# Two-layer hybrid trunk step: the input projection by pairs of weight tiles, with 512 latent columns in one matmul

## The chip, the cores and the metric

One core of a Trainium2 chip runs the whole program, a step of two layers, in one launch. The metric is the device time in microseconds (us); lower is better. TensorE (PE) multiplies matrices from SBUF into PSUM, which has 8 banks of 512 fp32 values per partition; ScalarE (ACT), VectorE (DVE) and GpSimd (POOL) do the element-wise work, and SyncE (SP) issues most of the loads. Every engine runs its own instructions strictly in the order in which the program wrote them, and waits on semaphores for the others.

## What is computed

Each layer takes 640 tokens (128 of a new prompt, 512 latent ones) of width 2048, modulates them, projects them to 6656 columns, sends those through three branches (a bidirectional HGRN2 recurrence, windowed attention, a convolution module), gates them and projects back. Cut to what matters here:

```python
def trunk_layer(x, shift, scale, gate, w_in_l, w_out_l, ...):
    h = x * (1 + scale) + shift
    z = h @ w_in_l                                   # 2048 -> 6656
    aq, ak, av, ag, hq, hi, hff, hfb, hgate, ca, cb, cgate = split(z)
    att = attention(aq, ak, av)
    hg_out, s_fin = hgrn2_branch(hq, hi, hff, hfb, ...)
    cv_out = conv_branch(ca, cb, ...)                # GLU, 31 taps, LayerNorm, swish
    mix = concat([att * silu(ag), hg_out * silu(hgate), cv_out * silu(cgate)])
    return layer_norm(ALPHA * x + gate * (mix @ w_out_l))

def gates(hf, lb):                                   # in hgrn2_branch
    one_minus_f = (1 - lb) * sigmoid(-hf)
    logf = log1p(-minimum(one_minus_f, 1 - GATE_EPS))
    return one_minus_f, logf
# A = q k exp(G_t - G_s) in each chunk; the state goes on with k * exp(g_last - G)
```

`shift`, `scale` and `gate` come from `silu(c) @ ada_w`, a product of one vector per request with a matrix of 2048 x 6144 for each layer ("ada" below).

## The kernel before

The stream h lies in SBUF feature-major, split into two fp32r halves `HH` and `HL`. The 52 tiles of `w_in` (128 columns each, the list `NTILES`) are projected one after another: for each of the 16 slices k of the inner dimension three products (`wh` with HH, `wh` with HL, `wl` with HH), each as two matmuls with the same stationary weights, one over 256 columns (prompt and the first 128 latent tokens, L1173) and one over 384 (the other latent tokens, L1175), into a tile `z` of two PSUM banks. There are two such tiles and four single banks `m` for everything else. The result lies feature-major, 640 tokens wide, and one ScalarE activation empties it (`evac`): e_hf takes the sigmoid of a forget gate (L453) and then its Ln (L461), e_hi copies and transposes back to token-major, the others likewise.

The weights arrive in quarters of a tile (256 KB, SP queue), ScalarE writes their fp32r half and its negative (L290, L291), and a DMA of POOL adds the raw weights (`split_add`). These splits are written four quarters ahead of their use.

Nothing is scheduled at run time: Python generators (`active`) write the work of the branches, and between every two k slices of projection the program writes a few steps of them (`pump`). What a step writes on PE, ACT, DVE and POOL keeps this place for good. The layer begins with 16 tiles of HGRN2, head by head: `hff`, `hfb`, `hi`, `hq` of head j+1 are projected while the recurrence of head j (`hg_main`) is computed. Its part that matters here, in the order in which it stands: compact products on PE (L540), exponentials of the 8-step base for the two directions (L600 on DVE, then L602 and L603 on ACT), compact products of them (L540 again), exponentials for the chunk states (L636, L640, L644), transposes, two copies out of PSUM (L657), and the chunk-state matmuls (L664).

Layer 0 begins with a stretch in which the ada weights are streamed (`ada_pe`, 32 loads for scale and shift of both halves) while the first `NS` tiles are projected in steps of two k slices; the other ada products are formed on DVE between the projection's steps (L362), at `RATE` of them per step. Between the layers, the output projection of the last column group, the LayerNorm and the transposes of the next stream stand beside a first half of the next layer's first two tiles.

Of the kernel before, what the change touches and what calls it, by code (L numbers as in the profile page):

```python
# [45 lines left out]
WN = (0, 3, 4)  # L46
# [27 lines left out]
RATE = ((1.0, 0.85, 0.5, 1.2), (0.5, 0.5, 0.0, 0.8))  # L74
# [3 lines left out]
class Free:  # L78
# [8 lines left out]
    def put(self, *xs):  # L87
        self.f.extend(xs)

# [36 lines left out]
def trunk(ctx: ExitStack, tc: tile.TileContext, A: dict):  # L126
# [38 lines left out]
    zt = [psp.tile([P, 1024], F32, name=f"z{i}") for i in range(2)]  # L165
    mb = [psp.tile([P, 512], F32, name=f"m{i}") for i in range(4)]
    ZP = Free(zt)
    M = Free(mb)
# [55 lines left out]
    def zput(z):  # L224
        if isinstance(z, tuple):
            M.put(*z)
        else:
            ZP.put(z)

# [69 lines left out]
    def ada_pe(jobs, raws, after):  # L299
# [3 lines left out]
        for (part, nch), kq in tiles:  # L303
            while nxt < len(tiles) and raws:
                (p2, n2), k2 = tiles[nxt]
                r = raws.popleft()
                sync.dma_start(out=r, in_=A["adaw0"][p2, n2, k2])
                fly.append(r)
                nxt += 1
                if nxt == W0:  # L310
                    for i in range(NS):
                        w_load1(0, i, 0)
# [127 lines left out]
    def zsb(z):  # L440
        return z[:, 256:896]

    def e_hf(l, j, d, z):
# [9 lines left out]
        act.activation(kd, zsb(z), AF.Sigmoid, scale=-1.0)  # L453
        zput(z)
# [16 lines left out]
    def to_tokens(vT, v):  # L471
        b0 = yield from M.get()
        for c in range(4):
            pe.transpose(b0[:, 128 * c:128 * c + 128], vT[:, 128 * c:128 * c + 128], ident)
        act.copy(v[:, 0:512], b0)
        M.put(b0)
        b1 = yield from M.get()
        pe.transpose(b1[:, 0:128], vT[:, 512:640], ident)
        act.copy(v[:, 512:640], b1[:, 0:128])
        M.put(b1)  # L480

    def e_hi(l, j, z):
# [3 lines left out]
        if isinstance(z, tuple):  # L486
            act.copy(s[:, 0:256], z[0][:, 256:512])
            act.copy(s[:, 256:640], z[1][:, 0:384])
        else:
            act.copy(s[:, 0:T], zsb(z))  # L490
        zput(z)
        yield
        yield
        yield from to_tokens(s[:, 0:T], v)
        S.put(s)
        flags.add(("hi", l, j))

    def e_hq(l, j, z):
        yield from wait(("hgset", l, j))
        act.activation(hv(l, hgset[l, j])[2], zsb(z), AF.Silu)  # L500
        zput(z)
        flags.add(("hq", l, j))
        yield
# [244 lines left out]
    def e_ak(l, g, z):  # L748
# [5 lines left out]
        act.copy(kp, z[:, 256:384])  # L754
# [4 lines left out]
        act.copy(lat(s), z[:, 384:896].rearrange("p (a b) -> p a b", a=2))  # L759
        zput(z)  # L760
# [15 lines left out]
    def e_av(l, g, z):  # L776
        yield from wait(("hgdone", l, 2 + g), ("cache", l))
        s, vl = yield from S.getn(F32, F32R)
        act.copy(s[:, 0:T], zsb(z))
        zput(z)  # L780
# [7 lines left out]
        for c in range(4):  # L788
            pe.transpose(b[:, 128 * c:128 * c + 128], s[:, 128 + 128 * c:256 + 128 * c], ident)
        split(V[:, 0:512], vl[:, 0:512], b)  # L790
        M.put(b)
        b = yield from M.get()
        pe.transpose(b[:, 0:128], s[:, 0:128], ident)
        act.copy(vp, b[:, 0:128])
        M.put(b)
        S.put(s)
        pool.dma_start(out=A["nv"][l, g], in_=vp)
# [10 lines left out]
    def e_aq(l, h, z):  # L808
# [3 lines left out]
        act.copy(pq(l, h), z[:, 256:384])  # L812
        act.copy(s[:, 0:512], z[:, 384:896])
        zput(z)
# [185 lines left out]
    def e_cb(l, j, z):  # L1000
        s = yield from S.get()
        act.activation(s[:, 0:T], zsb(z), AF.Sigmoid)
        zput(z)
# [4 lines left out]
    def e_ca(l, j, z):  # L1008
# [6 lines left out]
        dve.tensor_tensor(u[:, 15:143], z[:, 256:384], s[:, 0:128], op=ALU.mult)  # L1015
        dve.tensor_tensor(u[:, 158:670], z[:, 384:896], s[:, 128:640], op=ALU.mult)
        zput(z)
# [76 lines left out]
    def e_gate(l, k, z):  # L1094
        s = yield from S.get()
        act.activation(s[:, 0:T], zsb(z), AF.Silu)  # L1096
        zput(z)
# [17 lines left out]
    wraw = {}  # L1115

    def w_load1(l, i, c):
        pump_until(lambda: RAW.f)
        r = RAW.take()
        sync.dma_start(out=r, in_=A["win"][l, i, c])  # L1120
        wraw[l, i, c] = r

    def w_load(l, i):
        for c in range(4):
            w_load1(l, i, c)
# [3 lines left out]
    def w_split(l, i, c, lo_eng=None, hi_eng=None):  # L1129
        pump_until(lambda: len(WH.f) >= 2)  # L1130
        hi, lo = WH.take(), WH.take()
        r = wraw.pop((l, i, c))
        if lo_eng == "dma":
            split_add(hi, lo, r, A["win"][l, i, c])
        else:
            split(hi, lo, r, lo_eng, hi_eng)
        wsp[l, i, c] = (hi, lo)
# [24 lines left out]
    def mm(l, i, z, ks, halves):  # L1162
        za, zb = (z[0][:, 256:512], z[1][:, 0:384]) if isinstance(z, tuple) else (z[:, 256:512], z[:, 512:896])
        za = za.rearrange("p (a b) -> p a b", b=P)
        zb = zb.rearrange("p (a b) -> p a b", b=P)
        for k in ks:
            hi, lo = wsp[l, i, k // 4]
            o = 128 * (k % 4)
            wh, wl = hi[:, o:o + 128], lo[:, o:o + 128]
            for n_, (w_, h_) in enumerate(((wh, HH), (wh, HL), (wl, HH))):  # L1170
# [8 lines left out]
    zs = [zt[0], zt[1], (mb[2], mb[3])]  # L1179
    M.f = deque(mb[0:2])  # L1180
    ZP.f.clear()
    for k in range(6):
        load_x0(k)
    def start_mm(n):
        for i in range(NS):
# [427 lines left out]
```

## Time and profile before

| | |
|---|---|
| time, median of 3 runs | 2254.14 us (2252.49 to 2255.09) |
| the profiled execution: its own time | 2252.99 us |
| its span in the trace | 2251.1 us |
| mean granted TensorE clock | 0.992 |
| PE busy | 97% (15854 instructions) |
| DVE, ACT, POOL busy | 65%, 51%, 27% |
| DMA, mean over the span | 179 GB/s |

The span is the time from the first to the last instruction in the trace of one profiled execution; 1.9 us of that execution's own time lie outside it. An engine's busy share counts the time in which at least one of its instructions ran. TensorE's matmuls overlap one another, so the duration of one in a row is longer than its distance to the next; distances between starts are what adds up.

### The profile page before, as it was taken

The numbers are of one execution on the slowest core, as the hardware profiler recorded it, in microseconds if no ns is written. First come the engines' busy times: TensorE is split into PE (matmuls) and PEld (weight loads), VectorE is DVE, ScalarE is ACT, GpSimd is POOL, SyncE is SP. The second block draws the span as 40 slices with busy tenths as digits, with TensorE's granted clock in tenths as the row PEclk, the third lists the DMA queues.
The fourth block names the chain that finished last, engine by engine and source line by source line (L and its number), as shares of the span: only waits on it lengthen the run. The fifth ranks groups of instructions, "written<-read, shape, count | busy, mean of one in ns | idle before, by whom it ended". The sixth has DMA issues, their size and how long they took to land.

```text
span 2251.1 us, 42122 instructions
## 1 busy us (share of the span) xinstructions
PE 2178.7 (97%) x15854; PEld 2077.2 (92%) x15854; DVE 1472.3 (65%) x3795; ACT 1142.6 (51%) x2047; POOL 616.0 (27%) x704
## 2 busy tenths in 40 slices
PE   6899999999999999999989999999999999999995
PEld 3699999999999999988989999999999999998895
DVE  2488889557669998676673666534655877234458
ACT  1177877546565335511165878764556543551111
POOL 0034334332222243300032344433222133330005
PEclk9999999999999999999999999999999999999998
DMA  9978787887777789964435777788776577685332
GB/s 371 400 191 203 184 200 188 206 218 182 170 159 170 190 193 229 272 197 135 118 130 135 160 173 163 158 193 186 162 153 129 114 170 157 144 196 178 96 97 103
DMA packets 210716, 403.60 MB, mean 179 GB/s; under 512 B 24816, under 2 KB 30672, under 8 KB 209872
## 3 DMA queue, kind: packets, MB, share of 16 engines
q1 hardware_dynamic: 138992, 271.85, 38.3%
q0 software_dynamic: 61600, 116.96, 30.3%
q10 hardware_dynamic: 9920, 12.10, 1.7%
q8 instruction: 124, 2.03, 0.4%
q14 instruction: 80, 0.66, 0.1%
HBM read 383.46 MB, written 12.11 MB: 176 GB/s over the span
## 4 chain that ended last, share of the span: by engine, by line
PE 77%; DVE 11%; DMA 4%; issue 3%; ACT 3%; POOL 1%; ACTq 0%; SPq 0%; DVEq 0%; POOLq 0%
PE z L1175 31%; PE z L1173 21%; PE z L1432 9%; PE m L1432 8%; DVE junk L362 4%; DMA x<-adaw 2%; PE m L948 2%; PE m L862 2%; PE m L916 1%; DMA s<-xT 1%; PE m L664 1%; DVE y1y L1414 1%; ACT s L1392 1%; DVE s L534 1%; DVE y1y L1415 0%
## 5 line engine op out<-in xcount | busy, mean ns | idle before, releaser
L1175 PE MATMUL z<-HH,wh 128*128 128x384 f32 x3296 | 1045.8, 338 | 0.0
L1173 PE MATMUL z<-HH,wh 128*128 128x256 f32 x3296 | 926.4, 283 | 1.6 <-DVE wh L287 0.9
L292 POOL DMA_DIRECT2D wh<-win x388 | 344.4, 933 | 1090.8 <-ACT wh L291 1021.5
L1173 PEld LDWEIGHTS z<-HH,wh 128*128 128x128 f32 x3296 | 619.4, 189 | 5.5 <-DVE wh L287 1.6
L1175 PEld LDWEIGHTS z<-HH,wh 128*128 128x128 f32 x3296 | 620.0, 188 | 1.5
L1175 PE MATMUL z<-HL,wh 128*128 128x384 f32 x1648 | 557.6, 338 | 0.0
L362 DVE SCALAR_TENSOR_TENSOR junk<-raw,s 128x256 bf16<-128x256 f32 x1024 | 503.8, 492 | 52.1 <-DMA raw<-adawD 24.4
L1173 PE MATMUL z<-HL,wh 128*128 128x256 f32 x1648 | 461.3, 280 | 0.0
L1173 PEld LDWEIGHTS z<-HL,wh 128*128 128x128 f32 x1648 | 311.0, 189 | 0.0
L1175 PEld LDWEIGHTS z<-HL,wh 128*128 128x128 f32 x1648 | 309.9, 188 | 0.0
L291 ACT ACTIVATE wh<-wh 128x512 fp32r<-128x512 f32 x400 | 253.1, 633 | 79.4 <-PE z L1175 68.4
L290 ACT CAST wh<-raw 128x512 fp32r<-128x512 f32 x400 | 244.0, 610 | 71.2 <-issue 36.2
L286 ACT CAST wh<-raw 128x512 fp32r<-128x512 f32 x136 | 83.0, 621 | 305.0 <-PE m L1432 156.6
L1027 DVE SCALAR_TENSOR_TENSOR s<-s,sm,s 128x655 f32<-128x655 f32 x240 | 231.2, 963 | 6.3
L1432 PE MATMUL z<-wh,HH 128*128 128x512 f32 (+1 forms) x640 | 182.0, 368 | 0.0
L1432 PE MATMUL m<-wh,HH 128*128 128x512 f32 (+1 forms) x640 | 173.8, 357 | 0.0
L287 DVE TENSOR_TENSOR wh<-raw,wh 128x512 fp32r<-128x512 f32 x138 | 92.6, 687 | 122.9 <-ACT wh L286 120.2
L1432 PEld LDWEIGHTS z<-wh,HH 128*128 128x128 f32 x640 | 116.1, 189 | 20.0
L1432 PEld LDWEIGHTS m<-wh,HH 128*128 128x128 f32 x640 | 114.1, 189 | 17.5
L1432 PE MATMUL z<-wh,HL 128*128 128x512 f32 (+1 forms) x320 | 117.7, 368 | 0.0
L1432 PE MATMUL m<-wh,HL 128*128 128x512 f32 (+1 forms) x320 | 114.3, 357 | 0.0
L1096 ACT ACTIVATE s<-z 128x640 f32<-128x640 f32 x32 | 22.5, 703 | 151.6 <-PE z L1175 142.8
(555 smaller groups left out, 2745.2 us busy)
## 6 DMA issues: line engine op xcount, KB each, us to landing
raw<-win SPq DMA_DIRECT2D x416, 256.0 KB, 4.2
wh<-win POOLq DMA_DIRECT2D x388, 256.0 KB, 5.5
raw<-adawD SPq DMA_DIRECT2D x256, 256.0 KB, 4.0
x<-adaw SPq DMA_DIRECT2D x64, 512.0 KB, 8.3
raw<-wout SPq DMA_DIRECT2D x128, 256.0 KB, 2.8
s<-crow SPq DMA_DIRECT2D x32, 256.0 KB, 5.9
s<-xT ACTq DMA_DIRECT2D x16, 320.0 KB, 7.1
s<-s ACTq DMA_DIRECT2D x80, 64.0 KB, 3.8
```

The source lines that it names most:

```text
L286: act.copy(hi, src)
L287: (lo_eng or dve).tensor_tensor(lo, src, hi.bitcast(F32), op=ALU.subtract)
L290: act.copy(hi, r)
L291: act.activation(lo, hi.bitcast(F32), AF.Copy, scale=-1.0)
L292: pool.dma_start(out=lo, in_=w.bitcast(F32R), accum_op=ALU.add)
L362: dve.scalar_tensor_tensor(junk, r[:, 256 * n:256 * n + 256], 1.0, rows[0][:, 256 * c:256 * c + 256], op0=ALU.mult, op1=ALU.mult, accum_ou ...
L862: pe.matmul(b[:, 0:w], lhsT=a_, rhs=k_, start=(n_ == 0), stop=(n_ == 2))
L948: pe.matmul(o, lhsT=v_, rhs=p_, start=(y == 0 and n_ == 0), stop=(y == len(bl) - 1 and n_ == 2))
L1027: dve.scalar_tensor_tensor(acc, u[:, t:t + AW], sm[:, cw + t:cw + t + 1], acc, op0=ALU.mult, op1=ALU.add)
L1173: pe.matmul(za, lhsT=w_, rhs=h_[:, 0:2, k, :], start=st_, stop=sp_)
L1175: pe.matmul(zb, lhsT=w_, rhs=h_[:, 2:5, k, :], start=st_, stop=sp_)
L1432: pe.matmul(bs[tt][:, 0:w], lhsT=h_[:, tt, k, :], rhs=w_[:, o:o + w], start=(k == 0 and n_ == 0), stop=(k == KT - 1 and n_ == 2))
```

## The change

The 52 tiles become 26 pairs. For each k slice and product there are now three matmuls: one over all 512 latent columns for each tile of the pair (L1228), and one of 256 columns for both tiles' prompt part, in which the prompt tokens (`HH[:, 0, k]`) are the stationary operand and the weights of both tiles are streamed (L1231). So the prompt comes out token-major. `Pair.fill` copies those 256 columns out of PSUM on ACT (L243), and two steps later PE transposes each tile's half back (L249), but for `hi` and `av`, which want it token-major anyway. Every evacuation is written twice, for 512 latent and 128 prompt columns. PSUM is one queue of 8 banks. The weights are packed by quarters of two k slices and 256 columns. Layer 0 starts with two pairs beside the ada stream (before: three tiles), layer 1 with one pair; two entries of RATE rise.

```diff
-RATE = ((1.0, 0.85, 0.5, 1.2), (0.5, 0.5, 0.0, 0.8))
+RATE = ((1.0, 0.85, 0.6, 1.3), (0.5, 0.5, 0.0, 0.8))
+    class Pair:
+        def fill(self):
+            cs = yield from S.get()
+            act.copy(cs[:, 0:256], self.c)
+            self.cput()
+            yield
+            yield
+            self.T = yield from M.get()
+            for t in self.need:
+                pe.transpose(self.T[:, 128 * t:128 * t + 128], cs[:, 128 * t:128 * t + 128], ident)
...
     def e_hf(l, j, d, z):
...
-        act.activation(kd, zsb(z), AF.Sigmoid, scale=-1.0)
-        zput(z)
+        act.activation(kd[:, 128:T], z.lat, AF.Sigmoid, scale=-1.0)
+        z.put_lat()
+        zp = yield from z.prompt()
+        act.activation(kd[:, 0:128], zp, AF.Sigmoid, scale=-1.0)
+        z.put()
...
-    def mm(l, i, z, ks, halves):
...
-                if 0 in halves:
-                    pe.matmul(za, lhsT=w_, rhs=h_[:, 0:2, k, :], start=st_, stop=sp_)
-                if 1 in halves:
-                    pe.matmul(zb, lhsT=w_, rhs=h_[:, 2:5, k, :], start=st_, stop=sp_)
+    def mm(l, p, z, ks, parts=(0, 1), lat=((1, 5),)):
...
+                if 1 in parts:
+                    for t in range(2):
+                        for a, b in lat:
+                            x = z.ab[t][:, 128 * (a - 1):128 * (b - 1)].rearrange("p (a b) -> p a b", b=P)
+                            pe.matmul(x, lhsT=w_[:, o + 128 * t:o + 128 * t + 128], rhs=h_[:, a:b, k, :],
+                                      start=st_, stop=sp_)
+                if 0 in parts:
+                    pe.matmul(z.c, lhsT=h_[:, 0, k, :], rhs=w_[:, o:o + 256], start=st_, stop=sp_)
-    NS = 3
+    NS = 2
...
-            mm(l + 1, 0, zt[0], range(KT), (0,))
+            head, rest = ((1, 3),), ((3, 5),)
+            mm(l + 1, 0, zs[0], range(8), lat=head)
             g = ln_next(TT - 1)
...
-            mm(l + 1, 1, zt[1], range(KT), (0,))
...
+            mm(l + 1, 0, zs[0], range(8, KT), lat=head)
+            for q in range(8):
+                mm(l + 1, 0, zs[0], (2 * q, 2 * q + 1), (1,), rest)
```

How this moves instructions is seen in the order in which they stand on an engine. On PE, in the steady part of layer 0 (before; z is the tile's PSUM pair, wh a quarter of the weights):

```order
L1173 MATMUL z_100<-HH,wh_235 128x256
L1175 MATMUL z_100<-HH,wh_235 128x384
L1173 MATMUL z_100<-HH,wh_238 128x256
L1175 MATMUL z_100<-HH,wh_238 128x384
L1173 MATMUL z_100<-HL,wh_238 128x256
L1175 MATMUL z_100<-HL,wh_238 128x384
```

and the same place of the changed kernel, where m_103 and m_99 are the latent banks of the two tiles and m_102 holds the prompt of both:

```order
L1228 MATMUL m_103<-HH,wh_314 128x512
L1228 MATMUL m_99<-HH,wh_314 128x512
L1231 MATMUL m_102<-wh_314,HH 128x256
L1228 MATMUL m_103<-HL,wh_314 128x512
L1228 MATMUL m_99<-HL,wh_314 128x512
```

Two tiles took four matmuls for a product, and now take three; in all PE has 14646 matmuls before and 12326 after, of which 92 are the new transposes L249, while the 12 that turned the prompt of `hi` and `av` are gone.

On ACT, in layer 1, while the recurrence of head 1 is computed and the gates of head 2 are emptied, between the exponentials of the chunk states and the copies L657 (before):

```order
L636 ACTIVATE s_8731<-h11gg 128x128 x4
L640 ACTIVATE s_12631<-h11gg 128x128 x4
L453 ACT_TABLE_LOAD
L453 ACTIVATE h10kt<-z_100 128x640
L290 CAST wh_235<-raw_246 128x512
L291 ACTIVATE wh_238<-wh_235 128x512
L644 ACT_TABLE_LOAD
L644 ACTIVATE aE_87<-h11gg 128x5
L645 ACTIVATE aE_87<-h11gg 128x5
L649 DMA s_9444<-st 128x128
L650 DMA s_7282<-st 128x128
L461 ACT_TABLE_LOAD
```

and in the changed kernel, where L680 and L684 are the old L636 and L640, L501 the sigmoid of a prompt part and L509 the Ln:

```order
L680 ACT_TABLE_LOAD
L680 ACTIVATE s_8286<-h11gg 128x128 x4
L501 ACT_TABLE_LOAD
L501 ACTIVATE h10kt<-m_106 128x128
L339 CAST wh_311<-raw_166 128x512
L340 ACTIVATE wh_418<-wh_311 128x512
L684 ACT_TABLE_LOAD
L684 ACTIVATE s_11425<-h11gg 128x128 x4
L509 ACT_TABLE_LOAD
L509 ACTIVATE s_11426<-s_11426 128x640
L501 ACT_TABLE_LOAD
L501 ACTIVATE h10kt<-m_106 128x128
```

Both gates of a head come out at the same time now, so their sigmoids and Lns stand between the exponentials. From the first base exponential (L602, now L646) to the copies (L657, now L701) ACT has 3 table loads before and 8 after, in five of the eight heads; for head 0 of layer 0 and for both heads 3 it has 6, and before 3 (2 for heads 3).

On PE, at the end of a layer's projection, before the first matmuls of the output projection (before: L1173 and L1175, then L1432):

```order
L1173 MATMUL z_99<-HH,wh_416 128x256
L1175 MATMUL z_99<-HH,wh_416 128x384
L1432 MATMUL m_101<-wh_417,HH 128x512
L1432 MATMUL m_101<-wh_617,HH 128x512
L1432 MATMUL m_101<-wh_417,HL 128x512
```

and now:

```order
L1228 MATMUL m_102<-HH,wh_6687 128x512
L1228 MATMUL m_106<-HH,wh_6687 128x512
L1231 MATMUL m_99<-wh_6687,HH 128x256
L249 MATMUL m_104<-ident,s_8286 128x128 x2
L1495 MATMUL m_105<-wh_6715,HH 128x512
```

The last pair's two transposes stand between the projection and the output matmuls (L1495), and they read what ACT copies out of PSUM after the pair's last matmul.

## Rows read from the trace of the kernel before

**Rows 1.** Page, busy time, share of the span and instructions of each engine.

```profile
PE 2178.7 (97%) x15854; PEld 2077.2 (92%) x15854; DVE 1472.3 (65%) x3795; ACT 1142.6 (51%) x2047; POOL 616.0 (27%) x704
```

**Rows 2.** Page, chain of work that ended last: shares of the span by engine.

```profile
PE 77%; DVE 11%; DMA 4%; issue 3%; ACT 3%; POOL 1%; ACTq 0%; SPq 0%; DVEq 0%; POOLq 0%
```

**Rows 3.** PE's waits: for what, us in total, times, longest.

```profile
PE m L317 <- DMA x<-adaw: 19.1, 15, 6.7
...
PE m L1385 <- ACT s L1392: 6.1, 6, 3.9
...
PE m L540 <- DVE s L607: 4.3, 5, 1.3
```

**Rows 4.** The chain in order of time: start us, us, what.

```profile
934.56 2.04 PE m L1432 x9
...
1120.43 5.76 PE m L1478 x48
...
1175.15 6.46 PE z L1173 x46
1181.61 16.64 PE z L1175 x96
```

**Rows 5.** The chain around 1271 us, the same columns: matmuls of 128 columns.

```profile
1270.81 1.79 PE m L664 x16
```

**Rows 6.** Windows of 20 us: busy us of each engine (instructions), granted clock, DMA share, GB/s.

```profile
80.00:100.00 20.00, 16.73 (x149) 11.58 (x147) 7.56 (x18) 3.75 (x6) 0.00 (x0) 0.83 1.02 401
100.00:120.00 20.00, 18.05 (x179) 14.53 (x179) 11.23 (x28) 5.54 (x10) 0.00 (x0) 1.00 0.92 354
700.00:720.00 20.00, 20.00 (x143) 19.95 (x142) 19.51 (x44) 8.24 (x15) 4.10 (x5) 1.00 0.81 195
1160.00:1180.00 20.00, 17.60 (x118) 16.57 (x118) 16.44 (x30) 15.29 (x43) 4.65 (x5) 0.84 0.54 188
```

**Rows 7.** Timeline of ACT in layer 1: start us, us, line, operation, operands [idle before].

```profile
1319.24 1.28 ACT L602 ACT_TABLE_LOAD   x1
1320.53 0.74 ACT L602 ACTIVATE s<-s 128x640 f32<-128x640 f32 x1
1321.30 0.74 ACT L603 ACTIVATE s<-s 128x640 f32<-128x640 f32 x1
1321.94 0.60 ACT L290 CAST wh<-raw 128x512 fp32r<-128x512 f32 x1
...
1329.32 1.28 ACT L453 ACT_TABLE_LOAD   x1
1330.62 0.71 ACT L453 ACTIVATE h10kt<-z 128x640 f32<-128x640 f32 x1
1331.22 0.61 ACT L290 CAST wh<-raw 128x512 fp32r<-128x512 f32 x1
...
1335.43 0.74 ACT L461 ACTIVATE s<-s 128x640 f32<-128x640 f32 x1
1336.08 0.60 ACT L290 CAST wh<-raw 128x512 fp32r<-128x512 f32 x1
...
1337.25 1.05 ACT L657 COPY s<-m 128x512 f32<-128x512 f32 x2
...
1339.39 0.25 ACT L667 COPY s<-m 128x128 f32<-128x128 f32 x1
```

**Rows 8.** Timelines of PE and DVE in the same stretch.

```profile
1315.75 0.92 PE L540 MATMUL m<-s,s 128*32 128x32 f32 x80
...
1338.09 1.95 PE L664 MATMUL m<-h11v,s 128*128 128x128 f32 x16
...
1317.91 0.51 DVE L544 COPY_PREDICATED zd<-cmask,m 128x320 f32<-128x320 uint8 x1
1318.32 0.81 DVE L600 TENSOR_TENSOR s<-h11gg 128x640 f32<-128x640 f32 x1
```

More of the change, by code (lines that the diff above doesn't have):

```diff
@@ L45 @@
 W0 = 4
-WN = (0, 3, 4)
 CY = 5
@@ L88, in put, with get @@
         self.f.extend(xs)
+class Banks(Free):
+    keep = 0
+    def get(self):
+        while len(self.f) <= self.keep:
+            yield BLOCK
+        return self.f.popleft()
 class Slots(Free):
@@ L164, in trunk @@
     mv = [new(f"mv{i}", [P, 4]) for i in range(2)]
[L165 to L168, printed above, removed]
+    mb = [psp.tile([P, 512], F32, name=f"m{i}") for i in range(8)]
+    M = Banks(mb)
     crow = drp.tile([8, 2, 256], F32, name="crow")
@@ L222, in trunk, with __init__, put_lat, prompt @@
     S.put(crs)
[L224 to L228, printed above, removed]
+    class Pair:
+        def __init__(self, l, i, ab, c, cput):
+            self.key = ("pr", l, i)
+            self.ab, self.c, self.cput, self.T, self.cs = ab, c, cput, None, None
+            self.need = [t for t in (0, 1) if NTILES[i + t][0] not in ("hi", "av")]
+            self.left = len(self.need)
+        def fill(self):
[7 more added lines that the diff above has]
+                pe.transpose(self.T[:, 128 * t:128 * t + 128], cs[:, 128 * t:128 * t + 128], ident)
+            if self.left == 2:
+                S.put(cs)
+            else:
+                self.cs = cs
+            flags.add(self.key)
+    class Half:
+        def __init__(self, pair, t):
+            self.pair, self.t, self.lat = pair, t, pair.ab[t][:, 0:512]
+        def put_lat(self):
+            M.put(self.pair.ab[self.t])
+        def prompt(self):
+            yield from wait(self.pair.key)
+            return self.pair.T[:, 128 * self.t:128 * self.t + 128]
+        def put(self):
+            self.pair.left -= 1
+            if not self.pair.left:
+                M.put(self.pair.T)
+        def tokens(self):
+            yield from wait(self.pair.key)
+            return self.pair.cs[:, 128 * self.t:128 * self.t + 128]
+        def put_tokens(self):
+            S.put(self.pair.cs)
     def load_consts():
@@ L310, in ada_pe @@
                 if nxt == W0:
-                    for i in range(NS):
-                        w_load1(0, i, 0)
+                    w_more(NS)
             if kq == 0:
@@ L485, in e_hi @@
         s = yield from S.get()
[L486 to L491, printed above, removed]
+        act.copy(s[:, 0:512], z.lat)
+        z.put_lat()
         yield
         yield
-        yield from to_tokens(s[:, 0:T], v)
+        b = yield from M.get()
+        for c in range(4):
+            pe.transpose(b[:, 128 * c:128 * c + 128], s[:, 128 * c:128 * c + 128], ident)
+        act.copy(v[:, 128:T], b)
+        M.put(b)
         S.put(s)
+        zt = yield from z.tokens()
+        act.copy(v[:, 0:128], zt)
+        z.put_tokens()
         flags.add(("hi", l, j))
@@ L811, in e_aq @@
         s, r = need[0:2]
-        act.copy(pq(l, h), z[:, 256:384])
-        act.copy(s[:, 0:512], z[:, 384:896])
-        zput(z)
+        act.copy(s[:, 0:512], z.lat)
+        z.put_lat()
+        zp = yield from z.prompt()
+        act.copy(pq(l, h), zp)
+        z.put()
         yield from rope(s, r, lambda t: t[:, 0:512], cos, sin)
@@ L1094, in e_gate @@
     def e_gate(l, k, z):
+        while k < 8 and len(S.f) < 3:
+            yield BLOCK
         s = yield from S.get()
-        act.activation(s[:, 0:T], zsb(z), AF.Silu)
-        zput(z)
+        act.activation(s[:, 128:T], z.lat, AF.Silu)
+        z.put_lat()
+        zp = yield from z.prompt()
+        act.activation(s[:, 0:128], zp, AF.Silu)
+        z.put()
         yield
```

238 lines of the change are left out of this document (117 added, 121 removed).

## The prediction

> **What bounds the kernel now.** I read the busy times first: PE runs 97% of the span, the next engine 65% [rows 1]. The chain of work that ended last agrees: 77% of it is PE [rows 2]. So the distance from one matmul to the next is the price of nearly everything, and what PE waits for is next. Its longest waits are for ada weights in the first 100 us and for the LayerNorm between the layers; a few us go to the HGRN compact products, which wait for DVE [rows 3]. The windows say where idle time is left: 3.27 of 20 us at 80 to 100 us, with the DMA at 401 GB/s and a share of 1.02, 1.95 in the next window, and 2.4 between the layers [rows 6]. In the middle of a layer there is none (20.00 of 20) [rows 6]. So the change is worth what it takes out of PE's stream in the steady part, less every wait that it makes there. For those I read the timeline of ACT at the one place where it ends just ahead of PE (below).
>
> **The pitch of the matmuls.** In runs without gaps, 48 matmuls of 256 columns take 5.76 us, 0.120 each; 96 of 384 take 16.64, 0.1733 each; 9 of 512 take 2.04, 0.2267 each [rows 4]. Two tiles now cost 2 x (0.120 + 0.1733) = 0.5867 us for each slice and product. After the change it is 2 x 0.2267 + 0.120 = 0.5733. The row for 256 columns is of the transposed kind already, weights streamed and tokens stationary, so the new form has a price from this trace. The three widths lie 13.3 ns above columns divided by 2.4 GHz, and one matmul in four is dropped: 13.3 ns. A pair has 16 x 3 = 48 products, and 24 pairs in layer 0 and 25 in layer 1 lie outside the two starts: 49 x 48 x 0.01333 = **-31.4 us**.
>
> The Trainium skill has another figure ("TensorE: Matmul & The Clock Gate", section "Back-to-back issue gap"): a warm gap of columns / 2.4 plus 2.5 ns. By it the saving would be 49 x 48 x 2.5 ns = 5.9 us. The rows are of this kernel's own fp32r matmuls and decide.
>
> **The transposes.** 92 come and 12 go; 16 matmuls of 128 columns take 1.79 us, 0.112 each [rows 5]: 80 x 0.112 = **+9.0**.
>
> **The start of layer 0.** Before, three tiles are projected beside the ada stream and the fourth after it, 48 x 0.2933 = 14.1 us. Now four lie beside it: a step of two slices costs 4 x 3 x 0.5733 = 6.88 us where three tiles cost 5.28, so 1.60 more in each of eight steps. The first five lie where PE has idle time for it (3.27 in one window of 20 us) [rows 6]; the last three, from about 100 us on, where PE is nearly full, I count: 4.8. The fourth tile's 1.05 MB now lands in the stretch where DMA is full, 2.6 us at 401 GB/s. 14.1 - 4.8 - 2.6 gives **-6.7** (bounds: -1.3 if all eight steps count, less the load not at all; -9).
>
> **Between the layers.** Before, the halves are 48 + 46 or so of 256 and 96 of 384 columns (6.46 and 16.64 us at the end) [rows 4]: 28.2 us by pitch; now 24 x 0.36 twice and 96 x 0.12, 28.8. But 8.64 instead of 5.76 us of it now stand ahead of the last token tile's transposes, where PE idles 2.4 us of a window at a granted clock of 0.84 [rows 6]. I let that idle time fill and pay 0.6: **-1.8** (0 to -3).
>
> **The end of a layer.** The last pair's two transposes stand between the projection and the output matmuls, and need ACT's copy of 256 columns first. A copy of 128 takes 0.25, one of 512 half of 1.05 [rows 7], so 0.35; with the last matmul's way out and the transposes I take 0.8, twice: **+1.6** (1 to 3).
>
> **ACT in the recurrence.** This is the cost that the diff doesn't show. In the stretch of rows 7 and 8 the compact products end at 1316.67, ACT starts the base exponentials at 1320.53 and ends the first of the two L657 copies at 1337.25 + 0.52 = 1337.77, and PE starts L664 at 1338.09 [rows 7, 8]. ACT is 0.3 us ahead; nothing is left. Its row from the first exponential to that copy is 17.24 us. In the changed order the same row holds five more table loads at 1.29 (1319.24 to 1320.53), 6.45; a second Ln, 0.65; two sigmoids of 512 and two of 128 in place of one of 640 (0.60), by the rows some 0.9 more; the copy L243, 0.35; and one weight split less, -1.17 [rows 7]. That makes 24.4. It can start earlier than before, since no load stands before the exponentials: after DVE's 0.51 + 0.81 at the earliest, where before DVE ended 2.46 us after the products [rows 8]. I take 1.5, as the second exponential's operand is late too. PE reaches the changed L664 after 33 products of 0.573, 10 transposes and the second compact products: 21.0 us. 1.5 + 24.4 - 21.0 = 4.9 us of waiting (bounds: 0 if ACT's row is shorter than its parts; 5.9 if DVE is as late as before). Five heads have eight loads: 24.5. Head 0 of layer 0 has six: 2.3. Heads 3 have six and one sigmoid and Ln less around them: I take 1 each. That is 28.8; the waits of the compact products for DVE, 4.3 [rows 3], lie in the same stretches and are swallowed: **+24.5** (0 to 31).
>
> ACT's loads are also what the Trainium skill warns of ("ScalarE: Activation LUTs", section "Table sets: the hidden batching unit"): batch calls by table set. The change does the opposite here. The same page ("What ACT_TABLE_LOAD costs") gives 2.66 us a switch, with a drain; the trace shows 1.28 and the next instruction 1.29 after its start [rows 7]. By the page the five loads would cost 6.9 us more in each of five heads, some 34 in all, and the time would be near 2282.
>
> **At nothing.** A pair takes four of eight banks and lasts 48 x 0.573 = 27.5 us, and its evacuations, some 2 us of ACT, have that long before the bank is wanted; without that cover they cost those 2 us a pair. Weight splits stay four quarters, 13.8 us, ahead of use; if ACT is late by more, PE waits for the weights, a part of the last rival. POOL has four transfers fewer. The faster ada rates move DVE work within a layer; they are hidden while DVE has room, also below.
>
> **The sum.** The profiled execution took 2252.99 us, 1.9 outside its span, and 1.2 under the median of the three runs. 2253.0 - 31.4 + 9.0 - 6.7 - 1.8 + 1.6 + 24.5 = **2248 us**. So most of what PE saves is given back where ACT becomes the bound of a stretch.
>
> **Rivals.**
> (a) *The cluster on ACT is hidden.* If ACT's waits are elsewhere and the table loads fall into time in which PE is far enough behind, the sum lacks its last term: 2224. For it speaks ACT's 51% [rows 1]; against it, that ACT has no idle time in the rows of that stretch and in-order engines can't move the loads. Halfway, with the second half of the stall taken up by idle time that I don't see, 2236. Chance 0.27.
> (b) *DVE is late in the convolution, and the kernel is slower.* In layer 0 DVE is busy 19.51 of 20 us there [rows 6], and ada goes from 0.5 to 0.6 products a step: 13 tiles are 104 steps, so some 10 more DVE steps of about 1 us each, with half a us of room in 20. The convolution's LayerNorm on PE follows DVE's last taps at ten slices, 17 us. If DVE's lag, which no row gives, passes that, each us beyond is a us of PE, up to the 10 to 15 added: 2258 to 2263; with the upper end of the ACT cluster (+6), 2268. It decides where DVE is more than 17 us behind. Speaks against it: layer 1 has no such rate, and no wait of PE for the taps is in the list now. Chance 0.17.
> (c) *The matmuls don't save.* If 512 columns cost more than in the output projection, or the gap is 2.5 ns as in the page's formula (the rows above say 13.3), the first term goes to -5.9 and the time to 2274. Chance 0.03.
>
> **The numbers.** The forecast has 0.53. Two tenths of a percent, 4.5 us, are about what a measurement of this kernel can tell from no change: faster is below 2249.6, slower above 2258.7. Around 2248 with 8 us either way (stall from 16 to 31, start and transition by 3), of 0.53 some 0.29 lies below, 0.19 within, 0.05 above. With (a) faster is 0.56; with (b) and (c) slower is 0.25; same is 0.19. The range leaves out little of (a) and the outer part of (b): 2225 to 2264; the forecast's own is 2240 to 2256.
>
> **What would show it.** The pitch: L1228 pairs 0.2267 apart and 0.120 for L1231. The start: the first matmul of the third pair comes some 7 us ahead of that of the fifth tile before. The cluster: in PE's waits a line L708 or L700 for ACT L701, some seven times, 4 to 6 us each, and in ACT's timeline eight loads without gap before it. The tail: L249 waiting for L243 twice, under 1 us. I am wrong if PE's waits for ACT sum to less than 10 us (then the time is near 2224 to 2234), or if a wait for DVE in the convolution or for POOL's weights of over 5 us appears.

## The result: slower by 76 us

| | before | after |
|---|---|---|
| time, median of 4 runs each on one chip | 2253.31 us (2252.43 to 2255.09) | 2329.47 us (2329.18 to 2332.48) |
| span of the profiled execution | 2251.1 us | 2327.6 us |
| PE idle in it (span less busy time) | 72.4 us | 116.4 us |
| mean granted TensorE clock | 0.992 | 0.983 |

The ratio is 1.034, interval 1.0322 to 1.0358. The change makes the kernel slower, and 2329 lies far outside the range forecast. Before, the span held 2178.7 us of busy PE [rows 1]; two rows of the page after, busy times and the shares of the chain, are

```profile
PE 2211.2 (95%) x13534; PEld 1882.6 (81%) x13534; DVE 1471.8 (63%) x3799; ACT 1172.8 (50%) x2165; POOL 621.3 (27%) x700
PE 59%; issue 16%; DVE 11%; POOL 7%; DMA 4%; ACT 3%; ACTq 0%; POOLq 0%; SPq 0%; DVEq 0%
```

PE's share of the chain falls from 77% [rows 2] to 59%, and those of POOL and of issue (time in which an engine waited for nothing that the profile shows) rise; a share is no price, so I go by PE's busy time and its waits. With 2320 instructions fewer, PE is busy 32.5 us longer and idle 44.0 us longer: 76.5, the whole difference of the spans. Each half needs a reason. First the idle half, PE's waits after (for what, us in total, times, longest):

```profile
PE m L708 <- ACT s L701: 20.4, 5, 4.3
PE m L584 <- DVE s L578: 15.8, 10, 2.2
PE m L365 <- DMA x<-adaw: 15.7, 13, 6.6
PE m L375 <- DVE s L371: 11.3, 16, 3.0
PE m L1448 <- ACT s L1455: 5.2, 4, 3.9
PE m L617 <- DVE s L578: 5.2, 4, 3.9
PE m L700 <- DVE s L690: 3.5, 1, 3.5
PE m L475 <- DVE s L336: 2.8, 1, 2.8
PE m L249 <- ACT s L243: 2.6, 2, 2.2
```

L708 is the old L664, the chunk-state matmuls, and waits for ACT in five heads, as forecast. L617 and L584 are products of the four exponential levels that stand ahead of the base exponentials; they wait 21.0 us for DVE's L578, the old L534. In the same list of before the products L540 waited 4.3 for L607, which belongs to the base exponentials [rows 3], and 5.0 for L534:

```profile
PE m L540 <- DVE s L534: 5.0, 4, 1.4
```

That is 9.3 in all. L607 is now L651, and no wait for it is left. The waits of the ada stream (L365, L375) fell by 4 us. One wait for DVE does lie in the convolution: L475's 2.8 us, at 912.8 us, is for the second LayerNorm sum of layer 0, behind a split on DVE (L336) that takes 4.13 us there. No wait for POOL's weights is in the list.

Now the busy half. PE's timeline in layer 0, in a stretch without a wait (start us, duration us):

```profile
859.72 0.28 PE L1231 MATMUL m<-wh,HH 128*128 128x256 f32 x1
859.85 0.63 PE L1228 MATMUL m<-HL,wh 128*128 128x512 f32 x2
860.31 0.28 PE L1231 MATMUL m<-wh,HL 128*128 128x256 f32 x1
860.43 0.63 PE L1228 MATMUL m<-HH,wh 128*128 128x512 f32 x2
```

From one L1231 to the next is 0.59 us (0.586 over many products), where I had forecast 0.5733 and two tiles took 0.5867 before. Three matmuls now take what four took. The saving didn't come, but nothing was lost by it either. The rest of the busy half is seen in windows of 50 us, the same columns as rows 6, from layer 1's and layer 0's recurrence; before, the granted clock was 1.00 in each of them, with PE busy 50.00, 50.00 and 48.04. The first of the three before:

```profile
1300.00:1350.00 50.00, 50.00 (x515) 49.18 (x514) 34.38 (x78) 39.59 (x65) 20.24 (x24) 1.00 0.77 168
```

and all three after:

```profile
1300.00:1350.00 50.00, 45.56 (x243) 39.42 (x242) 24.04 (x64) 39.48 (x64) 15.01 (x19) 0.93 0.65 142
1350.00:1400.00 50.00, 44.71 (x394) 38.09 (x393) 31.97 (x73) 40.24 (x65) 19.27 (x22) 0.93 0.64 138
150.00:200.00 50.00, 41.97 (x375) 35.38 (x374) 40.65 (x106) 33.62 (x59) 17.24 (x20) 0.90 0.68 166
```

Fine windows over one wait show the order of events:

```profile
1310.00:1315.00 5.00, 1.93 (x11) 1.38 (x9) 3.05 (x8) 4.93 (x8) 0.00 (x0) 1.00 0.10 28
1315.00:1320.00 5.00, 3.77 (x17) 3.77 (x18) 2.85 (x8) 3.04 (x7) 2.29 (x3) 0.55 0.75 167
1320.00:1325.00 5.00, 5.00 (x22) 4.11 (x21) 3.89 (x13) 4.86 (x8) 1.33 (x2) 0.76 0.61 148
1325.00:1330.00 5.00, 5.00 (x39) 4.69 (x38) 0.08 (x1) 0.96 (x4) 1.02 (x2) 1.00 0.99 234
```

PE idles first, at a clock of 1.00; then it works again, at 0.55 and 0.76, and at 1.00 from 1325. From 130 us to PE's last matmul the trace of after has stretches granted 1.2 GHz of 61.4 us in sum (15 of them, five at L708's waits), and that of before 6.8. In the first 130 us, beside the ada stream, before has another 10.2 and after none, so over the whole run it is 61.4 to 17.1. At half speed, 44 us more of these cost up to 22. By the busy time it is 32.5 less 9.0 for the 80 transposes, so about 23.5; the last 1 to 2 us of that I can't place.

### The profile page after: what moved, and what is told of

Its sections match the earlier page's. It is cut to its first block, busy times and chain, and to the rows that moved or that the text cites. A ratio compares the mean times of both kernels' runs of the same rounds, so it can differ in the third digit from the quotient of the medians.

```text
span 2327.6 us, 37655 instructions
## 1 busy us (share of the span) xinstructions
PE 2211.2 (95%) x13534; PEld 1882.6 (81%) x13534; DVE 1471.8 (63%) x3799; ACT 1172.8 (50%) x2165; POOL 621.3 (27%) x700
## 4 chain that ended last, share of the span: by engine, by line
PE 59%; issue 16%; DVE 11%; POOL 7%; DMA 4%; ACT 3%; ACTq 0%; POOLq 0%; SPq 0%; DVEq 0%
PE m L1228 29%; PE m L1495 16%; PE m L1231 7%; DVE junk L410 3%; POOL wh L341 3%; DMA x<-adaw 2%; PE m L995 2%; PE m L909 1%; POOL s L565 1%; DVE s L578 1%; POOL s L568 1%; PE m L963 1%; PE m L365 1%; DVE s L1079 1%; DVE y1y L1477 1%
## 5 line engine op out<-in xcount | busy, mean ns | idle before, releaser
L1228 PE MATMUL m<-HH,wh 128*128 128x512 f32 (+1 forms) x3392 | 1042.3, 396 | 1.1 <-DVE wh L336 1.1
L341 POOL DMA_DIRECT2D wh<-win x384 | 337.8, 942 | 1165.6 <-ACT wh L340 972.3
L1228 PEld LDWEIGHTS m<-HH,wh 128*128 128x128 f32 x3392 | 533.5, 190 | 74.2 <-DVE wh L336 2.2
L1228 PE MATMUL m<-HL,wh 128*128 128x512 f32 (+1 forms) x1696 | 529.4, 393 | 0.0
L1231 PE MATMUL m<-wh,HH 128*128 128x256 f32 x1664 | 475.0, 285 | 1.1 <-DVE wh L336 1.0
L1231 PEld LDWEIGHTS m<-wh,HH 128*128 128x128 f32 x1664 | 314.5, 189 | 72.2 <-DVE wh L336 2.7
L1495 PE MATMUL m<-wh,HH 128*128 128x512 f32 (+1 forms) x1280 | 354.5, 364 | 0.0
L1228 PEld LDWEIGHTS m<-HL,wh 128*128 128x128 f32 x1696 | 265.2, 190 | 38.1
L1495 PEld LDWEIGHTS m<-wh,HH 128*128 128x128 f32 x1280 | 230.9, 189 | 37.7
L1231 PE MATMUL m<-wh,HL 128*128 128x256 f32 x832 | 237.4, 285 | 0.0
L1495 PE MATMUL m<-wh,HL 128*128 128x512 f32 (+1 forms) x640 | 232.7, 364 | 0.0
L1231 PEld LDWEIGHTS m<-wh,HL 128*128 128x128 f32 x832 | 157.4, 189 | 35.2
L336 DVE TENSOR_TENSOR wh<-raw,wh 128x512 fp32r<-128x512 f32 x142 | 95.3, 687 | 123.3 <-ACT wh L335 123.3
L1495 PEld LDWEIGHTS m<-wh,HL 128*128 128x128 f32 x640 | 121.2, 189 | 18.9
L243 ACT COPY s<-m 128x256 f32<-128x256 f32 x52 | 18.8, 362 | 160.9 <-PE m L1231 151.6
L336 DVE TENSOR_TENSOR wh<-m,wh 128x512 fp32r<-128x512 f32 x64 | 37.0, 619 | 59.9 <-ACT wh L335 59.8
```

The lines of the kernel that those rows point to most:

```text
L336: (lo_eng or dve).tensor_tensor(lo, src, hi.bitcast(F32), op=ALU.subtract)
L341: pool.dma_start(out=lo, in_=w.bitcast(F32R), accum_op=ALU.add)
L1228: pe.matmul(x, lhsT=w_[:, o + 128 * t:o + 128 * t + 128], rhs=h_[:, a:b, k, :], start=st_, stop=sp_)
L1231: pe.matmul(z.c, lhsT=h_[:, 0, k, :], rhs=w_[:, o:o + 256], start=st_, stop=sp_)
L1495: pe.matmul(bs[tt][:, 0:w], lhsT=h_[:, tt, k, :], rhs=w_[:, o:o + w], start=(k == 0 and n_ == 0), stop=(k == KT - 1 and n_ == 2))
```

## The experiments

My theory after the result: PE is slower by three things, the matmuls (dearer in this mix than alone), the waits, and the clock behind the waits. Rivals for the first are the layout (the 512 latent columns of a slice lie in four pieces of 128, apart by strides), the exchange of roles (tokens stationary in one matmul of three) and, later, the PSUM bank. The rival for the clock is that a wait costs its own length and no more. Later runs ask what the waits for DVE come from, and whether any form of the change beats the kernel before. A and B in an expectation are the two answers to the question of that run. All ratios are against the kernel before on the same chip; its medians lie between 2253.3 and 2254.4 over the chips, so differences of times between two runs are good to about 1 us from that alone. Where a variant adds lines, its numbers run a few beyond those of after (L708 becomes L709 or L710, L584 becomes L585 or L586).

**e1_kmajor.** The two halves of the stream lie so that 512 latent columns are contiguous:

```diff
+HH = new("HH", [P, KT, TT, P], F32R).rearrange("p k t c -> p t k c")   # HL the same
```

> The changed kernel with the stream h laid out by slice k, so that the 512 latent columns of one slice are contiguous in SBUF; nothing else is changed. Theory A (strides): the missing 13 ns per product come from streaming 512 columns in four pieces 8 KB apart; then a product goes from 586 to 573 ns, and the time falls by 49 x 48 x 13 ns = 31 us, to 2298. Theory B (the switch between weights and tokens as the stationary operand costs it): the product stays at 586 ns and the time at 2329 (within 5).

2332.05 us (2329.52 to 2334.82), 1.0342 [1.0325, 1.036]; the product still takes 0.586 us. The layout isn't the cause.

**e2_joint.** Both gates of a head are emptied in one step: four sigmoids behind one table load, then both Lns.

```diff
-    def e_hf(l, j, d, z):
+    def e_hf(l, j, z0, z1):
...
+        for kd, z in zip(kds, (z0, z1)):
+            act.activation(kd[:, 128:T], z.lat, AF.Sigmoid, scale=-1.0)
...
+        yield
+        ss = yield from S.getn(F32, F32)
+        for d, (kd, s) in enumerate(zip(kds, ss)):
...
+            act.activation(u, u, AF.Ln, bias=1.0, scale=-1.0)
```

> The changed kernel with the two gates of a head emptied in one step: four sigmoids behind one table load, two Lns behind one, so that 4 table loads instead of 8 stand between the base exponentials and the chunk-state copies. Theory A (ACT's row of table loads makes PE wait, and PE's waits lower the clock behind them): the wait of L708 for the copies (20.4 us) vanishes, with it a good part of the later waits for DVE (21 us) and of the clock's loss in the HGRN stretch: 2270 to 2305. Theory B (the wait of L708 only covers other lateness, of POOL and DVE): the time stays above 2318.

2295.14 us (2294.65 to 2296.83), 1.0184 [1.0169, 1.0199]: 34.3 less than after. L708's wait for ACT is gone; busy PE falls by 9.8 us (2211.2 to 2201.4) and idle PE by 24.5. The waits for DVE stay, 20.9 us together, so they don't come from the table loads:

```profile
PE m L585 <- DVE s L579: 18.4, 12, 2.3
...
PE m L618 <- DVE s L579: 2.5, 4, 1.8
```

**e3_both.** e1 and e2 together.

> Both edits together, slice-major stream and joint gates. If strides and table loads are both causes and add up: 2239 to 2275. If only the table loads: 2270 to 2305. If neither: 2320 or more.

2294.91 us, 1.0183 [1.0167, 1.0198]: as e2.

**e4_before_kmajor.** The kernel before with the layout of e1.

> The kernel before with the slice-major stream alone. Theory A (strides): its pieces are two and three, and a pair of matmuls takes 293 ns where contiguous rows would take 120 + 173; so there is nothing to win: 2253, within 5. If instead every strided piece costs some 4 ns, the pair falls to 285 and the time by 4992 x 8 ns = 40 us, to 2213.

2254.35 us, 0.9998 [0.9989, 1.0008]. The layout does nothing for the old form either, as expected there.

**b1_pitch.** A bench of matmuls alone (it leaves out the whole trunk step, as b2 and b3 do). Each block repeats one pattern 96 times without a wait; `c` is the 256-wide product:

```diff
+    for i, k in enumerate(KS):
+        pe.matmul(ab[0], lhsT=w0, rhs=HH[:, 1:5, k, :], **f(i, 96))
+        pe.matmul(ab[1], lhsT=w1, rhs=HH[:, 1:5, k, :], **f(i, 96))
+        pe.matmul(c, lhsT=HH[:, 0, k, :], rhs=wh[:, 0:256], **f(i, 96))   # L168; w0 in the place of HH: L178
```

> No trunk step: one load, then eight rows of matmuls with nothing else on the chip, for their distances alone (L162: 192 of 512 columns, weights stationary; L164: 96 of 256, tokens stationary, weights streamed; L166 to L168: 96 times 512, 512, 256 as the changed kernel has them; L171 to L174: the same in groups of six and three; L176 to L178: 512, 512, 256 with weights stationary throughout; L180 to L182: 512, 256, 512; L184, L185: 256 and 384 as before; L187: 96 of 512 with tokens stationary). Theory A (exchanging the roles of weights and tokens costs it): L162 goes at 227 ns, L164 at 120, the triple L166 to L168 at 586, the grouped one near 577, the one with weights stationary throughout at 573. Theory B (512 columns of h cost more than 512 of the weights by themselves): L162 at 230 or more, and both triples at 580 or more.

The view of one line's instructions gives duration in ns (least, median, most) and the first and the last start:

```profile
L164 PE MATMUL m<-wh,HH x96: 277/283/283, 101.6 to 113.0; 128*128 128x256 f32 x96
...
L168 PE MATMUL m<-wh,HH x96: 277/285/285, 113.5 to 169.3; 128*128 128x256 f32 x96
...
L174 PE MATMUL m<-wh,HH x96: 274/277/278, 170.8 to 224.9; 128*128 128x256 f32 x96
...
L178 PE MATMUL m<-wh x96: 285/285/285, 225.5 to 281.3; 128*128 128x256 f32 x96
```

95 distances lie between first and last start. L164, 256 columns alone: 11.4 / 95 = 0.120 us. L168, the kernel's product: 55.8 / 95 = 0.587. 512 columns alone take 0.2268. So the parts are priced as rows 4 have it and sum to 0.5733, and still the mix takes 13 ns more. (256 beside 384, as before the change, take 27.9 / 95 = 0.294, as their parts.) With the weights stationary in all three (L178) it is the same, so it isn't the exchange of roles. Six of 512 and then three of 256 (L174's block) take 0.58 a product: 54.1 less the last group's 0.24, over 93 products. Neither answer was right as it stood: 512 isn't dearer alone, and the roles don't matter; widths side by side do.

**e5_grouped.** e2 with that order in the kernel:

```diff
+            for n_, w_, h_, st_, sp_ in prods:
                 if 1 in parts:
                     pe.matmul(x, ...)
+            for n_, w_, h_, st_, sp_ in prods:
                 if 0 in parts:
                     pe.matmul(z.c, ...)
```

> The kernel of e2 with the three products of a slice in another order: six matmuls of 512 first, then the three of 256 with the tokens stationary, so that the roles are exchanged twice in a slice and not six times. Theory A (the exchange costs 6 to 7 ns each time): four of six go, 26 ns a slice, 16 x 49 x 26 ns = 20 us: 2275 (2270 to 2280). Theory B (the width costs it): 2295 within 5.

2282.65 us (2280.47 to 2284.07), 1.0123 [1.0106, 1.014]: 12.5 less than e2, and between the two answers. Busy PE fell by 17.8 (some 15 by b1's pitch: 49 x 48 x 6.5 ns) and idle PE rose by 6.1, so a third of the busy time that the order saves is waited away.

**e6_parity.** e2, with each weight split written one slice later. In after, the DMA that adds the raw weights (L341, issued by POOL) stands between POOL's subtractions for the last two exponential levels (L565, L568); before, and in seven of e6's eight heads, it doesn't, and one stands between the first two levels instead.

```diff
                 if k % 2:
                     WH.put(*wsp.pop((l, 8 * p + k // 2)))
-                    ahead(8 * p + k // 2)
+                    late.append(8 * p + k // 2)
+                else:
+                    for q in late:
+                        ahead(q)
+                    late.clear()
```

> The kernel of e2 with each weight split written one step later (before the pump of the next even slice), which moves it out from between the POOL subtractions of the last two levels, where e2 has it and the kernel before does not. Theory A (POOL's subtractions stand behind a weight DMA that waits for ACT, and DVE and PE's L585 behind them): the wait of L585 for DVE (18.4 us) falls to 8 or less, and the clock's loss with it: 2275 to 2288. Theory B (DVE or ACT are late there by themselves): 2292 or more.

2283.30 us (2279.72 to 2283.53), 1.0125 [1.011, 1.014]: 11.8 less than e2. POOL's timeline ahead of a compact product, after:

```profile
1278.93 1.59 POOL L565 TENSOR_TENSOR s<-h10gg 128x640 f32<-128x640 f32 x1
1280.16 1.67 POOL L568 TENSOR_TENSOR s<-h10gg 128x640 f32<-128x640 f32 x1
1284.07 0.88 POOL L341 DMA_DIRECT2D wh<-win  x1 [2.24 <-DVE s L578]
1284.67 1.56 POOL L565 TENSOR_TENSOR s<-h10gg 128x640 f32<-128x640 f32 x1
```

and in e6:

```profile
1260.58 1.59 POOL L566 TENSOR_TENSOR s<-h10gg 128x640 f32<-128x640 f32 x1
1261.80 1.66 POOL L569 TENSOR_TENSOR s<-h10gg 128x640 f32<-128x640 f32 x1
1263.11 1.57 POOL L566 TENSOR_TENSOR s<-h10gg 128x640 f32<-128x640 f32 x1
1264.32 1.72 POOL L569 TENSOR_TENSOR s<-h10gg 128x640 f32<-128x640 f32 x1
```

Second level after first: 4.51 us later there (1280.16 to 1284.67), 1.31 here (1261.80 to 1263.11). PE's waits in e6:

```profile
PE m L585 <- DVE s L579: 8.4, 8, 1.7
...
PE m L709 <- ACT s L702: 4.8, 4, 1.9
PE m L1227 <- DMA wh<-win: 4.1, 4, 2.9
```

With L613's 2.2 the products' waits for DVE are 10.6, near the 9.3 of before. Most of this gain of 10.3 is lost to the two new waits of 8.9, so idle PE falls by 2.6 only; busy PE falls by 9.1. The clock goes with that: the stretches at 1.2 GHz between 130 us and PE's last matmul fall from 41.0 us in e2 to 17.1, while those in the first 130 us, beside the ada stream, rise from 10.2 to 23.9.

**b2_widths.** The bench with other mixes.

> Again matmuls alone, weights stationary throughout, for the distances of mixed widths (L162: 512 throughout; L167, L168: 512, 256; L170, L171: 512, 384; L173, L174: 512, 128; L176 to L178: 384, 384, 256; L180 to L183: 512, 512, 256, 256; L185: 384 throughout; L187, L188: 256, 128). Alone, widths cost columns / 2.4 GHz + 13.3 ns each. Theory A (a narrower matmul after one of 512 loses some 13 ns, whatever comes between): 512, 256 takes 360 instead of 347 ns, 512, 384 takes 413 instead of 400, 512, 128 takes 293 instead of 280, and 512, 512, 256, 256 takes 707 instead of 693; 384, 384, 256 takes its 467. Theory B (any change of width costs it): 384, 384, 256 takes 480 too, and 256, 128 takes 200 instead of 187 - against it, the 256, 384 pairs of the kernel before take no more than their parts. Theory C (three matmuls in a turn cost it, not two or four): 512, 256 takes 347, 384, 384, 256 takes 480.

Read as in b1, in ns, with the sum of the parts alone in brackets (128 columns at 112, rows 5): 512 + 256: 353 (347); 512 + 384: 407 (400); 512 + 128: 340 (339); 256 + 128: 231 (232); 384 + 384 + 256: 467 (467); 512 + 512 + 256 + 256: 697 (693). So there is a surcharge of 3 to 13 ns where 512 stands beside 256 or 384, and none for 384 beside 256. The two mixes with 128 add up if a matmul of 128 costs here what it costs at L664; no bench has 128 alone. By the expectation's columns / 2.4 + 13.3 it would be 67, and both mixes would lie some 45 ns over their parts (293, where the expectation has 280 by a slip, and 187). No rule of mine gives the sizes.

**e7_gp.** e5 and e6 together.

> e2 with both later edits: products grouped by width within a slice (e5) and splits one step later (e6). If the two are apart (pitch; POOL's order), their gains of 12.5 and 11.8 us add up: 2271 (2267 to 2275). If the grouped order's gain is eaten by waits on ACT and DVE because PE runs ahead: 2277 or more.

2274.55 us (2273.74 to 2278.99), 1.0094 [1.0077, 1.0111]: near what was expected, with some of it waited away. The waits for ACT (7.4 us) and for the weights' DMA (6.1) are now as long as that for DVE (7.7).

**e8_quarter.** e7 with twelve of 512, then six of 256, for two slices:

```diff
-                mm(l, p, z, (k,))
+                mm(l, p, z, (k,), (1,))
                 if k % 2:
+                    mm(l, p, z, (k - 1, k), (0,))
```

> e7 with the products grouped by two slices: 12 of 512 columns, then 6 of 256. One change of width in six products instead of three: 13 ns x 49 x 8 = 5 us less than e7, if the width is what costs (2266, within 4); the same as e7 if it isn't.

2275.30 us, 1.0092 [1.0077, 1.0107]; a miss. Busy PE fell by 7.2 (2180.2 to 2173.0), idle PE rose by 5.8.

**e9_fill.** The changed kernel, with 18 matmuls put ahead of L708 in five heads, whose result is thrown away. They take PE's time while it would wait; the clock alone can gain.

```diff
             b = yield from M.get()
+            if d == 0 and (l, j) in ((0, 1), (0, 2), (1, 0), (1, 1), (1, 2)):
+                for _ in range(18):
+                    pe.matmul(b..., lhsT=HH[:, 0, 0, :], rhs=HH[:, 1:5, 0, :], start=True, stop=True)
             for i, c in enumerate(cs):
```

> The changed kernel with 18 matmuls of 512 columns (4.1 us), whose results are thrown away, ahead of L708 in the five heads in which PE waits there for ACT's copies (20.4 us in all): PE works where it waited, and nothing that is waited for comes earlier or later. Theory A (the waits themselves cost the granted clock, 1.2 GHz for some us behind each): the five stretches at the lower clock behind L708 go, and some 8 to 10 us with them: 2320 (2316 to 2325). Theory B (the clock falls for another reason, or the lost clock lies in time in which PE waits anyway): the time stays at 2329, or rises by up to 5.

2320.19 us (2318.91 to 2320.79), 1.0293 [1.0276, 1.031]: 9.3 less, for 90 matmuls more, which work for 20.4 us. Busy PE rose by 12.8 only, so the rest of its work got 7.6 shorter. PE's timeline at L708 in after, and the same place in e9 (L712):

```profile
1316.23 3.78 PE L708 MATMUL m<-h10v,s 128*128 128x128 f32 x16 [4.30 <-ACT s L701]
```

```profile
1308.15 4.28 PE L709 MATMUL m<-HH 128*128 128x512 f32 x18
1312.61 2.05 PE L712 MATMUL m<-h10v,s 128*128 128x128 f32 x16 [0.18 <-ACT s L701]
```

The same sixteen matmuls take 2.05 us in place of 3.78, and over the five heads 10.0 in place of 17.9. That the clock behind a wait costs time, beside the wait itself, is shown by this run: some 8 of the 9.3 us, for five waits. The stretches at 1.2 GHz fall from 61.4 to 47.8 us.

**e10_ln.** e8 with the Lns one step later, which leaves three table loads in the stretch of five heads:

```diff
             z.put()
         yield
+        yield
         ss = yield from S.getn(F32, F32)
```

> e8 with the Lns of the gates one step later, behind the exponentials of the chunk ends, so that 3 table loads instead of 4 stand between the base exponentials and the chunk-state copies, as many as in the kernel before. If PE's waits there (9.0 us) are ACT's loads: they fall below 3, and the time to 2268 (2264 to 2271). If they are ACT's other work (the copies, the split sigmoids): 2273 to 2277.

2266.51 us (2264.41 to 2268.12), 1.0056 [1.0041, 1.0071], as expected; the wait for ACT fell from 9.0 to 3.9, not below 3. It is the fastest version with pairs, and 0.6% slower than the kernel before. Its busy PE is 2176.4 us, 2.3 less than before, its idle PE 88.4, 16.0 more.

**b3_pieces.** The bench once more: weights of 64 columns, both 512s in one bank, other widths.

> Matmuls alone once more, variants of 512, 512, 256 (587 ns; its parts alone 573): L168 to L170 as it was; L172 to L174 with weights of 64 columns instead of 128; L176 to L178 with both matmuls of 512 into one PSUM bank; L180 to L182 with 448 columns instead of 512 (parts alone 2 x 200 + 120 = 520); L184 to L186 with 320 instead of 256 (600); L188: 256 alone (120); L190: 256 alone with weights of 64. Theory A (the next weights can't be loaded in the time of a matmul of 256): with 64 columns of weights the triple falls to 573, and with 320 it takes 600. Theory B (a full bank, or the change between banks): with one bank or with 448 columns the 13 ns go, with 64 columns of weights they stay. Theory C (any odd third matmul beside wider ones): all variants keep 13 ns.

```profile
L170 PE MATMUL m<-wh x96: 277/285/285, 103.4 to 159.1; 128*128 128x256 f32 x96
...
L174 PE MATMUL m<-wh x96: 277/278/282, 159.7 to 214.1; 128*64 128x256 f32 x96
...
L178 PE MATMUL m<-wh x96: 277/285/285, 214.7 to 270.4; 128*128 128x256 f32 x96
```

The product takes 55.7 / 95 = 0.586 us (L170), 0.573 with stationary weights of 64 columns (L174), 0.586 with one bank less (L178). So the change of bank between the two 512s isn't the cause, and the width of the stationary weights has a part in it. The record of their load lasts 187 ns with 128 columns and 134 with 64, but that it is the load is not shown: 256 columns alone also get cheaper with weights of 64 columns (10.8 / 95 = 0.114 for 11.4 / 95 = 0.120), 512 alone wasn't run with them, and so some of the surcharge may be left in the 0.573. With 128 columns, 448, 448, 256 take 0.527 where the parts by columns / 2.4 + 13.3 would take 0.520, and 512, 512, 320 take 0.607 for 0.600: half the surcharge, which no rule of mine gives.

**e11_hgonly.** e10 with the later splits only in the HGRN2 tiles.

> e10 with the weight splits one step later in the HGRN tiles alone, where POOL's subtractions are. If PE's waits for late weights elsewhere (2.9 us at 899 us, 0.4 to 0.8 at some others) come from the later splits, 3 to 5 us go: 2262 (2260 to 2265). If from DMA: 2266.

2271.21 us (2269.01 to 2274.87), 1.0085 [1.0068, 1.0101]: a miss. The wait for the weights' DMA fell from 5.2 to 0.8 us, but 1.9 at L475, 1.9 at L428, 1.5 at L586 and 0.8 at L249 came back, and busy PE rose by 3.2.

## Why the prediction was wrong

By the spans, the forecast was -5 and the result +76.5: 81.5 us to explain.

**The pitch: this step failed (31.4 us).** "After the change it is 2 x 0.2267 + 0.120 = 0.5733." Each price was right, as b1 shows, but I added prices that were each measured in a run of one width. In the mix the product costs 0.586, and the saving is nil. The one mix in the trace of before, 256 beside 384, does add up (0.294 in b1 too), and I took it that any mix would. Rival (c), "the matmuls don't save", had the outcome at a chance of 0.03, but not the reason: it put the cost into one matmul of 512, and that costs no more (0.2268). Why the mix is dearer stays open.

**The granted clock: a term that the sum lacked (up to 22 of about 23.5 us).** I priced each wait at its own length. The stretches at 1.2 GHz are 44 us longer than before. That they cost is shown by e9 (some 8 us for the five waits at L708) and, with the waits going at the same time, by busy PE in e2 (-9.8) and e6 (-9.1); the 23.5 for the whole is worked out from the busy times, no run alone shows it. A sign of it was in the rows that I had: two of the three windows with idle time had 0.83 and 0.84 [rows 6].

**DVE's waits ahead of the level products: a term that the sum lacked (16.0 us, and 4.2 at L700).** I priced only the 4.3 us for L607 and let them be swallowed, and they did vanish. The other wait of the same products, 5.0 for L534, I passed over; it rose to 21.0. e6 shows the cause by its effect: with the split's DMA out of POOL's place between the last two levels, e2's 20.9 becomes 10.6. I had looked at POOL's transfers ("four transfers fewer") and not at where they stand in its order, which is what e6 changes. e6 moves the ACT half of the split as well, and I didn't part the two. L700's 4.2 are of head 0 of layer 0 alone; no run was made on them.

The three make 75.1 of the 81.5 (31.4 + 23.5 + 16.0 + 4.2). The remainder is a balance of small terms: L708's wait fell short of my 28.8 by 8.4, and waits at L475, L909, L428 and the tail, with a smaller gain in the waits between the layers, made more than up for it.

**Right: the cluster on ACT.** This is ACT's timeline at one head, with five of the eight loads that I counted:

```profile
1291.35 0.74 ACT L646 ACTIVATE s<-s 128x640 f32<-128x640 f32 x1 [0.64 <-DVE s L644]
...
1295.72 1.28 ACT L498 ACT_TABLE_LOAD   x1
...
1299.29 1.28 ACT L680 ACT_TABLE_LOAD   x1
...
1301.88 1.28 ACT L501 ACT_TABLE_LOAD   x1
...
1304.65 1.28 ACT L684 ACT_TABLE_LOAD   x1
...
1312.50 1.28 ACT L509 ACT_TABLE_LOAD   x1
...
1315.61 1.05 ACT L701 COPY s<-m 128x512 f32<-128x512 f32 x2
```

From 1291.35 to the end of the first copy, 1315.61 + 0.52 = 1316.13, is 24.8 us; 24.4 was forecast. The waits are 20.4 in five heads, 4.1 each for 4.9; heads 0 of layer 0 and heads 3 have none of note. The next instruction starts 1.29 after a load here too, so the sum by rows, without a drain, was the one to use. e2, with four loads, has no such wait left. What I had as the price of the cluster was the wait only; with the clock behind it, it is near 30 (20.4 and e9's 9.3), and e2 got back 34.3.

**The start of layer 0 was right:** the third pair's first matmul comes at 131.7 us where the fifth tile's came at 139.6, 7.9 earlier, for -6.7. **The tail:** two waits of L249 for L243, 2.6 in all for a term of 1.6; one of them was 2.2 and not under 1. **Between the layers** PE's wait for the LayerNorm fell from 6.1 to 5.2, by 0.9 for a term of 1.8. **Rival (b)** (DVE late in the convolution) came in one place and small: L475's 2.8 us in layer 0, not 10 to 15. Ahead of it two DVE instructions took about 4 us each while POOL computed beside them; that isn't the lag of the taps that I had in mind.

## What to carry to other kernels

A matmul's price from a run of one shape needn't hold in a mix of shapes (0.586 for 0.573 here): before you build on fewer, wider matmuls, run the exact sequence as a bench, which costs one kernel. Price a wait of TensorE at more than its length where the windows show a lower clock behind it, and test that by filling the wait with throw-away matmuls. When code is written in another order, read the order on each queue that a moved instruction passes: here a DMA issue between two of POOL's computations held the second (4.51 us for 1.31).

## What the runs showed of the hardware

- A product of 512, 512 and 256 columns takes 13 ns more than its parts alone (0.586 us for 0.573); with stationary weights of 64 columns it takes 0.573. The rule behind it stays open after three benches.
- Eighteen throw-away matmuls in each of five waits made the kernel faster (2329.5 to 2320.2 us).
- After a subtraction on POOL, its next DMA issue came 2.23 to 2.25 us later in 12 of 18 such places between 1180 and 1700 us of after, whichever engine was named as what it waited for. With the 0.60 from there to the next subtraction, a DMA between two of them costs some 2.8 us there.
- Some of DVE's ada products, 0.43 us as a rule, take over 3 us where POOL's subtractions run beside them; in the same stretch as the rows of POOL above:

```profile
1278.70 3.42 DVE L410 SCALAR_TENSOR_TENSOR junk<-raw,s 128x256 bf16<-128x256 f32 x1
...
1284.44 3.44 DVE L410 SCALAR_TENSOR_TENSOR junk<-raw,s 128x256 bf16<-128x256 f32 x1
```

They end at 1282.12 and 1287.88, 0.3 us after POOL's second subtraction each time (1281.83 and 1287.60). The kernel before has such places too (32 of 1024 products over 1 us, 20 of 1024 after), so they don't explain the difference; no run was made on them.
